# The two ends, the v stage and the u seam of a hybrid RG-LRU / gMLP block: shorter roots, diagonals on ScalarE, constants at the start, operands by tile

## The chip, the cores and the metric

One core of one Trainium2 chip runs the kernel. The metric is the device time of one execution in microseconds (us). A measurement gives the median of several executions.

## The reference, cut to what matters

Batch 1, 1024 tokens, model width 1024, one layer, all in float32:

```python
h = rms_norm(x, norm_mix_g)
rnn_x, rnn_gate, sgu_u, sgu_v, gate_a, gate_b = split(h @ w_in)
rnn_x = causal_depthwise_conv(rnn_x, conv_w, conv_b)
y_a = gelu(rnn_gate) * rg_lru(rnn_x, ...)       # decay = exp(-8 r softplus(-lam))
y_b = gelu(sgu_u) * (tril(w_s) @ layer_norm(gelu(sgu_v)) + b_s)   # chunks of 128 tokens
merged = sigmoid(gate_a) * (y_a @ w_proj_a) + sigmoid(gate_b) * (y_b @ w_proj_b)
x = x + merged @ w_out
g, u = split(rms_norm(x, norm_ffn_g) @ w_gate_up)
x = x + (silu(g) * u) @ w_down
return rms_norm(x, norm_final_g)
```

## The kernel before, in words

**Products.** Each float32 operand is split into a high part, rounded to float32r by ScalarE (ACT, line 93), and a low part, the rest, by VectorE (DVE, line 94). A product is three matmuls on TensorE (PE): high by high, high by low, low by high (`mm3`, lines 97 to 99). The large products after the v stage use a Strassen-Winograd scheme (`wino`, line 232): seven products M1 to M7 of blocks of 512, whose operands A11, A12, A22, S1 to S4 are blocks of the input and sums of them.

**Order of the work.** Weights come through a queue of loads (`start_loads`, line 128, on SyncE's DMA queue, SP) and splits (`pump`, line 136). `state["limit"]` bounds how far it runs and `state["ahead"]` how many splits ahead of their use are made. From line 564 to line 787 the order on PE, ACT, DVE, POOL and SP is the written one (`manual_schedule`). Elsewhere a list scheduler sets it, and `later(n, fn)` puts work n steps on. Every engine and queue works in order, so an instruction that waits holds all behind it.

**Start (lines 567 to 597).** SP loads x transposed (`xt`) in pieces of 256 tokens, the first of them in halves of 128 tokens, and the weights of v's first half, `wv0`. ACT issues the load of `pv`, the small parameters. Twelve warm-up matmuls run on PE. x is scaled by the gain and split (`x_split`); 1/rms of a row is applied later.

**v, first half (lines 594 to 649).** Eight tiles t of 128 tokens, each 24 matmuls. `x_rms` (line 490) makes 1/rms of a pair of tiles from sums of squares, by `rstd_early` (line 394): a root by bits and three Newton steps. `x_diag` (line 495) writes 1/rms on a diagonal, the high parts by ACT (line 500) and the low ones by DVE (line 501), `x_row` (line 505) broadcasts it by a matmul with ones, and `scale_x` (line 513) multiplies x by it. `ws_split` and `ws_sums` prepare the spatial weights. `v0_done` applies Gelu and takes statistics.

**v, second half (lines 708 to 740).** Eight tiles again. Per tile: 24 matmuls with `wv1`, Gelu (line 658), statistics on DVE (line 659). Tiles are grouped as 0, 1-2, 3-4, 5-6, 7. With the last tile of a group come `v_norm` (the root) and `v_centre` (ACT, line 678). Two tiles later `v_split` (lines 684, 685) makes the halves `vn`, `v_mix` multiplies them by the spatial weights (lines 696, 697), ACT copies one part from PSUM (line 699), DVE adds the other (line 705), and SP stores the result to `mix_d` in four pieces of 128 KB. Between these stand the operands of the u products: `scale_x` of x's second half with tiles 0 and 1, `sums` (lines 550 to 552) with tiles 2 and 4, `part` with tiles 1, 2, 4, 5, 6, `sum_s4` with 6 and 7.

**u seam (lines 763 to 786 and 858 to 872).** The first products M1, M2, M5, M6 of u0 and u1 (`head`) alternate with the last two tiles of `v_split` and `v_mix`, with the S2 and S4 parts. S3 and A22 follow outside the written order, and there too the recurrence constants (lines 876 to 892): `lam` is loaded by SP, ACT takes Abs and Exp (line 880), DVE 17 instructions of 128x8.

**After that** come the recurrence and gate products (`rnn_pair`, `gate_pair`), the projections, the feed-forward block and the down product. In the down product (line 1343 on) M4 is the last; after its k loop the four tiles i get their last four k one after the other, and each is then added to x (line 1300), squared (line 1308), multiplied by the gain (line 1310), scaled by its root (`finish`, line 1312) and stored by SP (line 1322). `square` of the second halves comes by `later(8, ...)`.

Of the kernel before, what the change touches and what calls it, by code (L numbers as in the profile page):

```python
# [14 lines left out]
P = 128  # L15
# [13 lines left out]
RG_C = 8.0  # L29

# [21 lines left out]
def block_kernel(ctx: ExitStack, tc: tile.TileContext, a: dict, out: bass.AP):  # L52
# [75 lines left out]
    def start_loads(upto=None):  # L128
        while state["load"] < min(upto or len(loads), state["loads"]) and (state["load"] < 2 or left[state["load"] - 2] == 0):
            ld = loads[state["load"]]  # L130
            ld[2] = wpool.tile([P, 4, HALF], F32, name=f"wraw{state['load']}", tag="wraw")
            for k in range(4) if state["load"] < 2 else (slice(0, ld[1]),):
                nc.sync.dma_start(ld[2][:, k], ld[0][:, k])
# [243 lines left out]
    act.activation(small.tile([P, 1], F32, name="warm", bufs=1), eps_t, AF.Gelu_apprx_tanh)  # L377
# [16 lines left out]
    def rstd_early(pool_, var, scale, name, n=1, y=None):  # L394
# [5 lines left out]
        dve.tensor_scalar(h, var, -0.5 * scale, -0.5 * EPS, ALU.mult, ALU.add)  # L400
        dve.tensor_scalar(y.bitcast(I32), h.bitcast(I32), -0.5, float(0x5F3759DF - 2 ** 22 - 2 ** 30),
                          ALU.mult, ALU.add)
# [56 lines left out]
    with tc.tile_pool(name="phv", bufs=1) as wk:  # L459
# [35 lines left out]
        def x_diag(q):  # L495

            dg = dgs[q] = wk.tile([P, 2, 2, P], F32R, name=f"dg{q}", tag="vb", bufs=3)
            for i in range(2):
                r = rms[:, 2 * q + i:2 * q + i + 1]
                act.activation(dg[:, 0, i], ident, AF.Copy, scale=r)  # L500
                dve.scalar_tensor_tensor(dg[:, 1, i], ident, r, dg[:, 0, i].bitcast(F32), ALU.mult, ALU.subtract)
# [36 lines left out]
        def part(name, src, i):  # L538

            ks = slice(2 * i, 2 * i + 2)  # L540
# [26 lines left out]
        act.dma_start(pv, a["pv"])  # L567
        first, second = slice(0, P), slice(P, 2 * P)
# [873 lines left out]
```

## Time and profile before

| | us |
|---|---|
| median of 3 runs (lowest, highest) | 1420.47 (1419.41, 1421.47) |
| the profiled execution | 1419.23 |
| its span, first to last instruction | 1417.5 |
| PE busy | 1397.0 (99%) |
| PE loading weights, beside it | 1151.0 |
| DVE busy | 1100.7 |
| ACT busy | 792.9 |

Times in rows count from the start of the span. PE's clock has two levels, 2.4 and 1.2 GHz, shown as a granted clock of 1.00 and 0.50. A matmul's row is longer than the distance to the next one, because matmuls are pipelined. "Idle before" is the time that the engine stood before an instruction, with what released it.

### The profile page before, as it was taken

The numbers are of one execution on the slowest core, as the hardware profiler recorded it, in microseconds if no ns is written. First come the engines' busy times: TensorE is split into PE (matmuls) and PEld (weight loads), VectorE is DVE, ScalarE is ACT, GpSimd is POOL, SyncE is SP. The second block draws the span as 40 slices with busy tenths as digits, with TensorE's granted clock in tenths as the row PEclk, the third lists the DMA queues.
The fourth block names the chain that finished last, engine by engine and source line by source line (L and its number), as shares of the span: only waits on it lengthen the run. The fifth ranks groups of instructions, "written<-read, shape, count | busy, mean of one in ns | idle before, by whom it ended". The sixth has DMA issues, their size and how long they took to land.

```text
span 1417.5 us, 17185 instructions
## 1 busy us (share of the span) xinstructions
PE 1397.0 (99%) x6216; PEld 1151.0 (81%) x6216; DVE 1100.7 (78%) x1807; ACT 792.9 (56%) x1320; POOL 75.0 (5%) x59
## 2 busy tenths in 40 slices
PE   9998999999999999999999999999999999999997
PEld 7777888788888888888888788888888888888886
DVE  6999999988888889798656976666666664697595
ACT  8467688888889865443443543333333333444454
POOL 0000000000000000000000021111111111000000
PEclk9999999999999999999999999999999999999999
DMA  9323545433333388774611132222222226942342
GB/s 322 139 60 109 200 164 178 167 116 115 114 107 107 105 310 315 259 295 150 222 60 45 74 112 112 111 112 107 88 110 112 111 93 249 347 179 85 110 141 82
DMA packets 71045, 212.45 MB, mean 150 GB/s; under 512 B 6320, under 2 KB 20656, under 8 KB 58416
## 3 DMA queue, kind: packets, MB, share of 16 engines
q1 hardware_dynamic: 70816, 211.32, 41.7%
q8 instruction: 48, 0.79, 0.2%
q14 instruction: 37, 0.30, 0.1%
q10 hardware_dynamic: 144, 0.04, 0.0%
HBM read 148.68 MB, written 62.65 MB: 149 GB/s over the span
## 4 chain that ended last, share of the span: by engine, by line
PE 73%; DVE 13%; ACT 8%; DMA 2%; issue 2%; SPq 0%; DVEq 0%; ACTq 0%; POOLq 0%; POOL 0%
PE f_p L99 10%; PE f_p L97 10%; PE f_p L98 10%; PE d_M L97 5%; PE d_M L99 5%; PE d_M L98 5%; PE g_p L99 2%; PE g_p L98 2%; PE g_p L97 2%; PE pa_p L98 2%; PE pb_p L99 2%; PE pb_p L98 2%; PE pa_p L97 2%; PE pa_p L99 2%; PE pb_p L97 2%
## 5 line engine op out<-in xcount | busy, mean ns | idle before, releaser
L93 ACT ACTIVATE dl_M<-wraw 128x512 fp32r<-128x512 f32 x77 | 48.6, 631 | 105.0 <-PE d_M L99 92.3
L98 PE MATMUL d_M<-d_M,dl_M 128*128 128x512 f32 x264 | 102.8, 389 | 0.0
L97 PE MATMUL d_M<-d_M,dl_M 128*128 128x512 f32 x264 | 102.7, 389 | 0.0
L99 PE MATMUL d_M<-d_M,dl_M 128*128 128x512 f32 x264 | 102.7, 389 | 0.0
L93 ACT ACTIVATE f_t<-wraw 128x512 fp32r<-128x512 f32 x88 | 55.2, 630 | 84.0 <-PE f_p L99 64.1
L94 DVE TENSOR_TENSOR dl_M<-wraw,dl_M 128x512 fp32r<-128x512 f32 x77 | 54.0, 701 | 51.5 <-ACT dl_M L93 51.3
L94 DVE TENSOR_TENSOR f_t<-wraw,f_t 128x512 fp32r<-128x512 f32 x88 | 70.8, 805 | 23.1 <-ACT f_t L93 22.1
L97 PE MATMUL f_p<-f_S,f_t 128*128 128x512 f32 x176 | 68.6, 390 | 0.3 <-ACT f_t L93 0.3
L97 PE MATMUL f_p<-m,f_b 128*128 128x512 f32 x176 | 68.6, 390 | 0.0
L99 PE MATMUL f_p<-m,f_b 128*128 128x512 f32 x176 | 68.5, 389 | 0.0
L98 PE MATMUL f_p<-f_S,f_t 128*128 128x512 f32 x176 | 68.5, 389 | 0.0
L98 PE MATMUL f_p<-m,f_t 128*128 128x512 f32 x176 | 68.5, 389 | 0.0
L99 PE MATMUL f_p<-m,f_t 128*128 128x512 f32 x176 | 68.5, 389 | 0.0
L98 PE MATMUL f_p<-m,f_b 128*128 128x512 f32 x176 | 68.5, 389 | 0.0
L99 PE MATMUL f_p<-f_S,f_t 128*128 128x512 f32 x176 | 68.4, 390 | 0.0
L97 PE MATMUL f_p<-m,f_t 128*128 128x512 f32 x176 | 68.3, 389 | 0.0
L94 DVE TENSOR_TENSOR f_b<-wraw,f_b 128x512 fp32r<-128x512 f32 x66 | 47.2, 718 | 15.7 <-ACT f_b L93 15.0
L93 ACT ACTIVATE f_b<-wraw 128x512 fp32r<-128x512 f32 x66 | 41.0, 625 | 32.6 <-PE f_p L99 29.9
L98 PEld LDWEIGHTS d_M<-d_M,dl_M 128*128 128x128 f32 x264 | 49.5, 188 | 10.4 <-DVE d_M L94 0.2
L99 PEld LDWEIGHTS d_M<-d_M,dl_M 128*128 128x128 f32 x264 | 49.6, 188 | 10.4
L97 PEld LDWEIGHTS d_M<-d_M,dl_M 128*128 128x128 f32 x264 | 49.5, 188 | 10.3
L198 DVE TENSOR_TENSOR wraw<-wraw 128x512 f32<-128x512 f32 x50 | 53.0, 1060 | 1.1
(503 smaller groups left out, 4208.6 us busy)
## 6 DMA issues: line engine op xcount, KB each, us to landing
wraw<-in_w_gu_dram SPq DMA_DIRECT2D x22, 1024.0 KB, 5.0
wd<-in_w_down_dram SPq DMA_DIRECT2D x11, 1024.0 KB, 9.5
wraw<-in_w_r_dram SPq DMA_DIRECT2D x8, 1024.0 KB, 7.2
wraw<-in_w_g_dram SPq DMA_DIRECT2D x8, 1024.0 KB, 5.0
wraw<-ffs_d SPq DMA_DIRECT2D x8, 1024.0 KB, 5.1
wraw<-ffa_d SPq DMA_DIRECT2D x6, 1024.0 KB, 6.0
xn<-in_x_dram SPq DMA_DIRECT2D x8, 512.0 KB, 9.0
wraw<-in_w_u_dram SPq DMA_DIRECT2D x4, 1024.0 KB, 5.9
```

The lines of the kernel that those rows point to most:

```text
L93: act.activation(hi, src, AF.Copy)
L94: return (eng or dve).tensor_sub(lo, src, hi.bitcast(F32))
L97: pe.matmul(o, lh, rh, start=start, stop=False, **kw)
L98: pe.matmul(o, lh, rl, start=False, stop=False, **kw)
L99: pe.matmul(o, ll, rh, start=False, stop=stop, **kw)
L198: dve.tensor_sub(raw[:, 0], raw[:, 2], raw[:, 0])
```

## The change

- `rstd_early` takes two steps instead of three: an ordinary one and one of higher order; 9 instructions instead of 11 for a pair, 7 instead of 8 for one column.
- `x_diag` splits 1/rms itself (128x2) and ACT writes all four diagonals.
- `lam` is loaded by ACT's queue at the start, right behind `pv`. Abs and Exp stand there ahead of the Gelu warm-up activation, and DVE's 17 instructions behind `x_split(1)`.
- The first loads go weight, x, weight, x, in whole pieces of 256 tokens, and the split of a weight comes before that of x. Eight warm-up matmuls instead of twelve. The first two tiles go k by k.
- The operands are given to other tiles: `scale_x(1)` begins behind tile 6 of the first half; `sums` is cut into `sum_s1`, `sum_s3`, `sum_s2`, with tiles 1, 3 and 5; the S1 parts with tiles 4 and 6; `sum_s4` with tile 7 and in the seam. `v_split` goes by halves, and `mix_out` copies, adds and stores half a tile (256 KB) at a time.
- The seam is written out up to the A22 parts, with each weight split before its head (`ahead` 0).
- At the end the last tile's last four k run in two halves of 256 columns, with partial sums added before; the last root is written out; ACT's queue stores one half. `square` of the second halves comes by `later(5, ...)`.

Cut to its core:

```diff
@@ rstd_early @@
-        for _ in range(3):
-            ...
-            dve.scalar_tensor_tensor(y, t, 1.5, y, ALU.add, ALU.mult)
+        product()
+        dve.scalar_tensor_tensor(y, t, 1.5, y, ALU.add, ALU.mult)
+        product()
+        dve.scalar_tensor_tensor(t, t, 5.0 / 3.0, t, ALU.add, ALU.mult)
+        dve.scalar_tensor_tensor(y, t, 1.25, y, ALU.add, ALU.mult)
@@ x_diag @@
-            act.activation(dg[:, 0, i], ident, AF.Copy, scale=r)
-            dve.scalar_tensor_tensor(dg[:, 1, i], ident, r, dg[:, 0, i].bitcast(F32), ALU.mult, ALU.subtract)
+            split(hi, lo, rms[:, c])
+            for n, r in enumerate((hi.bitcast(F32), lo)):
+                for i in range(2):
+                    act.activation(dg[:, n, i], ident, AF.Copy, scale=r[:, i:i + 1])
@@ start @@
+    act.dma_start(pv, a["pv"])
+    act.dma_start(lam, a["lam"])
...
+        act.activation(lam_c[:, 0], lam, AF.Abs)
+        act.activation(lam_c[:, 0], lam_c[:, 0], AF.Exp, scale=-1.0)
+        act.activation(small.tile([P, 1], F32, name="warm", bufs=1), eps_t, AF.Gelu_apprx_tanh)
+        for j in range(2):
+            ...
+            for k in range(4):
+                nc.sync.dma_start(ld[2][:, k], ld[0][:, k])
+                if j == 0 and k < 2:
+                    xt_load(0, slice(k, k + 1))
+                elif k % 2 == 0:
+                    xt_load(0, slice(4 * j + k, 4 * j + k + 2))
...
-        for _ in range(12):
+        for _ in range(8):
...
-        for ks in (range(4), range(4, 8)):
+        for k in range(NK):
             for t in acc:
-                tm_half(acc[t], "wv0", H, t, ks)
+                tm_half(acc[t], "wv0", H, t, (k,))
...
+        recurrence_constants(wk)
         x_rms(0)
@@ second half of v @@
-            if t == 2:
-                sums(0)
+            if t == 1:
+                part("A11", block(0, 0, 1), 1)
+                sum_s1(0)
+                sum_s3(0)
+                sum_s2(0)
+            if t == 3:
+                sum_s1(1)
+                sum_s3(1)
             if t == 4:
-                part("S1", s1s[0], 0)
-                sums(1)
+                part_s1(0)
...
+            if t == NT - 1:
+                allow(2 * NK + 1)
+                allow(2 * NK + 2)
+                sum_s4(0)
+                part("A12", block(0, 1, 1), 1)
+                v_mix(t - 2)
+                for q in range(2):
+                    mix_out(t - 2, q)
+                    v_split(t - 1, q)
@@ seam @@
         head("u0")
+        pump(where["u0", "M2"] + 1)
         v_mix(6)
-        v_mixed(6)
-        v_split(7)
+        for q in range(2):
+            v_split(7, q)
+            mix_out(6, q)
+        pump(where["u1", "M2"] + 1)
         head("u1")
         take(2)
         head("u0")
+        sums13("u0", raw["u0"])
+        pump(where["u0", "M5"] + 1)
+        sum_s4(1)
+        sums13("u1", raw["u1"])
         v_mix(7)
...
@@ end @@
+    def end(part):
...
+        for i in range(2):
+            c = slice(i * HALF // 2, (i + 1) * HALF // 2)
+            b = ps(f"d_end{i}")[:, c]
+            part(b, c)
+            x = X2[t][:, c]
+            dve.tensor_add(x, x, b)
+            act.activation(b, x, AF.Square, accum_out=q[:, i:i + 1])
...
+        act.activation(o[:, hs(1)], X2[t][:, hs(1)], AF.Copy, scale=s[:, 3:4])
+        act.dma_start(out[ts(t), hs(1)], o[:, hs(1)])
+        dve.tensor_scalar(o[:, hs(0)], o[:, hs(0)], s[:, 3:4], None, ALU.mult)
+        nc.sync.dma_start(out[ts(t), hs(0)], o[:, hs(0)])
...
-            later(8, lambda: square(4 + i, 1))
+            later(5, lambda: square(4 + i, 1))
...
+            if m == "M4" and i == 3:
+                add(banks[c][3], NT - 1, 0)
+                end(part_of)
+                continue
```

## Rows read from the trace of the kernel before

**Rows 1.** Busy us by stretch, with instruction counts; last: PE clock, DMA share, GB/s.

```profile
core 0: us, PE busy (x) PEld busy (x) DVE busy (x) ACT busy (x) POOL busy (x), PEclk, DMA share, GB/s
...
6.40:19.10 12.70, 12.23 (x48) 8.72 (x49) 10.51 (x24) 10.21 (x26) 0.00 (x0) 1.00 1.06 362
...
20.00:54.00 34.00, 33.85 (x153) 27.80 (x152) 29.44 (x94) 24.72 (x53) 1.09 (x1) 1.00 0.62 226
54.00:122.00 68.00, 62.88 (x324) 52.23 (x323) 63.50 (x148) 44.51 (x83) 0.00 (x0) 1.00 0.26 86
122.00:146.00 24.00, 21.89 (x97) 17.63 (x96) 22.01 (x33) 17.23 (x29) 0.10 (x1) 0.93 0.47 143
...
142.20:145.50 3.30, 3.30 (x8) 2.62 (x9) 3.10 (x4) 3.07 (x6) 0.00 (x0) 0.50 0.57 169
...
146.00:260.00 114.00, 113.60 (x500) 93.41 (x499) 109.23 (x188) 86.28 (x127) 0.20 (x2) 1.00 0.56 187
```

**Rows 2.** Timeline of the start (start, us, engine, line); DMA issues, last column us to landing.

```profile
0.80 0.42 ACTq L567 DMA_DIRECT2D pv<-in_pv_dram  x1
...
1.42 4.94 PE L593 MATMUL warm<-ident 128*128 128x128 f32 x24 [1.42 <-POOL ident masks.py:199]
...
6.48 0.50 PE L97 MATMUL pv<-wv,h 128*128 128x512 f32 x1
...
pv<-in_pv_dram ACTq DMA_DIRECT2D x1, 40.0 KB, 2.0
lam<-in_lam_dram SPq DMA_DIRECT2D x1, 4.0 KB, 4.2
```

**Rows 3.** Timeline of the end: the last matmul and DVE behind it.

```profile
1408.41 0.39 PE L99 MATMUL d_M<-d_M,dl_M 128*128 128x512 f32 x1
...
1409.09 0.69 DVE L1310 TENSOR_TENSOR x<-x,g_fin 128x512 f32<-128x512 f32 x1 [0.64 <-ACT g_fin L1308]
...
1409.77 0.67 DVE L1300 TENSOR_TENSOR x<-x,d_M 128x512 f32<-128x512 f32 x1
```

**Rows 4.** Waits of PE: us in total, times, longest.

```profile
PE mx L697 <- DVE vn L685: 2.3, 4, 1.2
PE mx L696 <- ACT vn L684: 2.3, 2, 1.3
PE u_p L97 <- ACT u_t L93: 2.1, 1, 2.1
```

**Rows 5.** Timeline of tile 2 of v's second half, DVE and ACT.

```profile
71.52 0.69 ACT L658 ACTIVATE vb<-pv,rms 128x512 f32<-128x512 f32 x1 [2.59 <-PE pv L99]
...
72.02 1.22 DVE L550 TENSOR_TENSOR xs<-x 128x1024 f32<-128x1024 f32 x1
...
75.67 0.69 DVE L659 BATCH_NORM_STATS2 st<-vb 128x6 f32<-128x512 f32 x1
...
76.84 0.72 ACT L678 ACTIVATE va<-va,mv 128x512 f32<-128x512 f32 x1 [3.15 <-DVE mv L669]
```

**Rows 6.** The root of tiles 1 and 2 on DVE, first and last of 11.

```profile
76.72 0.16 DVE L400 TENSOR_SCALAR rv<-mv 128x2 f32<-128x2 f32 x1
...
78.68 0.16 DVE L409 SCALAR_TENSOR_TENSOR rv<-rv 128x2 f32<-128x2 f32 x1
```

**Rows 7.** The diagonals (busy, mean ns, idle before), and DVE's waits in the seam.

```profile
L501 DVE SCALAR_TENSOR_TENSOR dg<-ident,rms,dg 128x128 fp32r<-128x128 f32 x8 | 2.5, 347 | 1.1 <-ACT dg L500 1.1
...
L500 ACT ACTIVATE dg<-ident,rms 128x128 fp32r<-128x128 f32 x8 | 2.8, 394 | 9.1 <-DVE rms L409 9.1
...
DVE h_S L94 <- ACT h_S L93: 2.2, 4, 1.1
```

**Rows 8.** The constants' load on SP, and ACT's table load and Exp.

```profile
134.89 0.43 SPq L446 DMA_DIRECT2D lam<-in_lam_dram  x1
...
139.38 1.28 ACT L880 ACT_TABLE_LOAD   x1
140.67 0.21 ACT L880 ACTIVATE sp_e<-sp_e 128x8 f32<-128x8 f32 x1
```

**Rows 9.** Two matmuls of 256 columns, and the next one.

```profile
30.05 0.40 PE L511 MATMUL rms<-dg,ones 128*128 128x256 f32 x2
30.28 0.39 PE L97 MATMUL pv<-wv,h 128*128 128x512 f32 x1
```

More of the change, by code (lines that the diff above doesn't have):

```diff
@@ L131, in start_loads @@
             ld[2] = wpool.tile([P, 4, HALF], F32, name=f"wraw{state['load']}", tag="wraw")
-            for k in range(4) if state["load"] < 2 else (slice(0, ld[1]),):
-                nc.sync.dma_start(ld[2][:, k], ld[0][:, k])
+            nc.sync.dma_start(ld[2][:, :ld[1]], ld[0][:, :ld[1]])
             state["load"] += 1
@@ L376, in block_kernel, with recurrence_constants @@
     make_identity(nc, ident)
[L377 removed]
+    lam = const.tile([P, 8], F32, name="lam")
+    lam_c = const.tile([P, 2, 8], F32, name="lam_c")
+    act.dma_start(pv, a["pv"])
+    act.dma_start(lam, a["lam"])
+    def recurrence_constants(wk):
+        sp = {n: wk.tile([P, 8], F32, name=f"sp_{n}") for n in ("z", "z2", "p")}
+        e = lam_c[:, 0]
+        dve.tensor_scalar(sp["z"], e, 2.0, None, ALU.add)
+        dve.reciprocal(sp["z"], sp["z"])
+        dve.tensor_mul(sp["z"], sp["z"], e)
+        dve.tensor_mul(sp["z2"], sp["z"], sp["z"])
+        dve.tensor_scalar(sp["p"], sp["z2"], 1.0 / 17, None, ALU.mult)
+        for c in (15, 13, 11, 9, 7, 5, 3):
+            dve.scalar_tensor_tensor(sp["p"], sp["p"], 1.0 / c, sp["z2"], ALU.add, ALU.mult)
+        dve.scalar_tensor_tensor(sp["p"], sp["p"], 1.0, sp["z"], ALU.add, ALU.mult)
+        dve.tensor_scalar(sp["z"], lam, -1.0, 0.0, ALU.mult, ALU.max)
+        dve.scalar_tensor_tensor(sp["p"], sp["p"], 2.0, sp["z"], ALU.mult, ALU.add)
+        dve.tensor_scalar(lam_c[:, 0], sp["p"], RG_C / 2, None, ALU.mult)
+        dve.tensor_scalar(lam_c[:, 1], sp["p"], -RG_C, None, ALU.mult)
     def par(name, f):
@@ L751, in block_kernel @@
         U = {n: wino(n, ops, *(call(n, i) for i in range(4)), order=LATE) for n in ("u0", "u1")}
-        state["ahead"] = 3
+        raw = {n: loads[queue[where[(n, "M1")]][0]][2] for n in U}
+        state["ahead"] = 0
         def head(n):
@@ L771, in block_kernel @@
         head("u0")
+        sums13("u0", raw["u0"])
+        pump(where["u0", "M5"] + 1)
+        sum_s4(1)
+        sums13("u1", raw["u1"])
         v_mix(7)
-        v_mixed(7)
-        part("S2", block(0, 0, 0), 0)
+        for q in range(2):
+            mix_out(7, q)
+        pump(where["u1", "M5"] + 1)
         head("u1")
-        part("S2", block(0, 0, 1), 1)
+        for i in range(2):
+            part("S2", block(0, 0, i), i)
+        sum2("u0", raw["u0"])
+        pump(where["u0", "M6"] + 1)
+        head("u0")
+        sum2("u1", raw["u1"])
+        pump(where["u1", "M6"] + 1)
+        head("u1")
+        take(4)
+        for i in range(2):
+            part("S4", block(0, 1, i), i)
+        head("u0")
+        head("u1")
+        state["ahead"] = 5
         take(2)
         head("u0")
-        head("u1")
-        part("S4", block(0, 1, 0), 0)
-        take(2)
-        part("S4", block(0, 1, 1), 1)
-        head("u0")
-        head("u1")
-        take(2)
+        a22 = [wk.tile([P, 2, HALF], F32, name=f"a22_{i}", tag="vn", bufs=2) for i in range(2)]
+        for i in range(2):
+            part("S3", block(1, 0, i), i)
+        for i in range(2):
+            act.activation(a22[i], block(1, 1, i), AF.Copy)
+        head("u1")
+        for i in range(2):
+            part("A22", a22[i], i)
         cur["defer"] = False
     ms.__exit__(None, None, None)
+    for fn in postponed:
+        fn()
+    postponed.clear()
     with tc.tile_pool(name="phr", bufs=2) as wk:
@@ L1353, in part, with part_of @@
                     stop and k == KD - 1, skip_group_check=True)
+        def part_of(b, cs):
+            for k in range(last, KD):
+                x, w = weight(("dn", m, k))
+                mm3(b, x[:, 0, ts(3)], x[:, 1, ts(3)], w[:, 0, cs], w[:, 1, cs], k == last, k == KD - 1)
         first = 2 if m == "M4" else 0
```

182 lines of the change are left out of this document (87 added, 95 removed).

## The prediction, made before the change was run

> **What bounds the kernel now.** I read the page's busy shares first: PE works 1397.0 of 1417.5 us, so only about 20 us can be won, and the table by stretch says where. From 146 us on PE is idle 0.4 us in 114 and a matmul of 512 columns comes every 0.227 us (113.6 us over 500) [rows 1]. Idle PE lies at three places. Before the first useful matmul: 6.48 us, in which only warm-up matmuls run [rows 2]. From 54 to 146 us: 68 less 62.88 and 24 less 21.89, 7.2 us in all; DVE is busy 63.50 of the 68, so PE stands because DVE is late. After the last matmul: 8.7 us (1408.80 to 1417.5) [rows 3]. The list of waits names the middle: 2.3 and 2.3 us for `vn`, the halves of the normalized v, and 2.1 us for a weight split of ACT [rows 4]. The last wait costs twice: TensorE's granted clock falls to 0.50, its 1.2 GHz level, for 3.3 us behind it [rows 1], which loses half of that, 1.65 us.
>
> **How the waits for `vn` arise.** ACT has `v1` of tile 2 by 72.2 us, yet DVE's statistics start at 75.67, because three 128x1024 operand passes stand ahead of them. ACT's centring waits 3.15 us for that, and the split of the next tile comes behind it [rows 5]. The root in between is 11 small instructions from 76.72 to 78.84, 0.195 us each [rows 6]. Tile 4 repeats the pattern.
>
> **The change, part by part.**
>
> *Middle (54 to 146).* The sums move from tiles 2 and 4, each of which closes a group, to tiles 1, 3 and 5, which don't: about 3.7 us of DVE work leaves the path from statistics to `vn`. `v_split` and `mix_out` go by half tiles in the last three tiles, so that PE can start on a half. Three pair roots go from 11 to 9 instructions (0.39 us each), two single ones from 8 to 7. Sixteen stores to `mix_d` of twice the size replace 32; on SP only the loads of the seam's `mix` stand behind them, which come later than before. What is to be won is 7.2 us of idle and 1.65 us of half clock, 8.9. Does DVE have the time? It had 63.5 us of work from 54 to 122; it loses 3 x 0.39 + 2 x 0.25 = 1.7 of roots and four 128x512 passes of `scale_x`, 2.8, that go ahead of the loop: 59.0 us into the 62.9 that PE needs. It fits, with 3.9 us for hand-overs. In the seam that follows, splits of operands waited for ACT 2.2 us in four such hand-overs, 0.55 each [rows 7]; I leave three of them on PE's path, 1.6 us. **Term: -7.3.** Ends: -8.9 if none is left, -3.5 if only the wait for ACT's split (2.1 with its 1.65, rounded down) goes.
>
> *Constants.* `lam` was loaded by SP at 134.89 and ACT waited for it, then reloaded its table for 1.28 at 139.38 [rows 8]; PE's 2.1 us wait above stands behind that and is already counted. The 17 small DVE instructions go to about 20 us: 17 x 0.195 = 3.3. From 20 to 54 DVE has 34 less 29.44, 4.6 us free [rows 1]. In come 3.3 and the 2.8 of `scale_x`; out go four roots (4 x 0.39 = 1.6) and eight `dg` passes of 0.347 (2.8, with 1.1 us of waits for ACT) [rows 7] against four tiny subtractions of 0.2. Net +2.5 of 4.6: covered, but the stage becomes full, and if that cover is gone the weights' low halves for the second loop are late; I set 0.3 us.
>
> *Diagonals.* ACT makes four 128x128 copies a pair instead of two: 8 x 0.394 = 3.2 us more, and four tiny ones of 0.2. ACT waited 9.1 us for the roots at this place [rows 7], which covers them: nothing. If DVE were not late there, they would stand ahead of a Gelu, 0.9 us a pair.
>
> *Start.* ACT now issues two DMAs (0.42 each), then waits for `lam`; behind that wait stand the Gelu table load (1.28), the warm activation and `ones` (0.2 and 0.3), and the first weight and x splits (0.63 and 0.5), for which PE and DVE wait. Where will `lam` land? `pv` on this queue took 2.0 us, `lam` on SP's 4.2 [rows 2]; issued at 1.3 it lands at 3.3 to 5.5. I take 3.6, near `pv`, the same queue at the same moment. Abs and Exp 0.4, then the chain above, 2.9: first matmul at 6.9 instead of 6.48. But x comes whole with each weight, so 48 matmuls need 48 x 0.2275 = 10.9 and some 0.6 for the first splits: done at 18.4. Before, the 48 took until 19.1 [rows 1], so -0.7. SP issues 11 loads in another order with the same bytes; queue and engines are the same. **Term with the 0.3: -0.4.** Ends: -1.3, and +3.2 with `lam` at 5.5 (first matmul 2.0 later, at 8.9) and 1.65 of half clock behind an idle PE.
> At the table load a page of the Trainium skill (ScalarE: Activation LUTs, "What ACT_TABLE_LOAD costs") states 1283 ns and a drain of about 1380 for every switch. The trace disagrees on the drain: Exp starts at 140.67, right after 139.38 + 1.28 [rows 8]. By the page the first matmul would come 1.4 us later and the term would be +1.0.
>
> *Recurrence stage (146 to 320).* It loses the 3.3 us of constants on DVE, but PE arrives some 8 us earlier and DVE had only 114 less 109.2, 4.8 us, free until 260 [rows 1]. 4.8 and 3.3 are 8.1: just enough. **Term: +0.5.** Ends: -1.0 (a wait or two fewer) and +3.0 (half of the 4.8 isn't usable, and a hand-over of 0.55).
>
> *End.* The last tile's last four k go in two column halves: 24 matmuls of 256 for 12 of 512, the same columns: two of 256 took 0.23 [rows 9], one of 512 0.227, so 0 (ends -0.1 and +0.5). Before, the add of the last bank started at 1409.77, 0.97 behind PE's end, because DVE had waited for a square of an earlier half [rows 3]; that square now comes three ticks sooner. A half's add, square and multiply save about 0.2 + 0.25; the root is 0.2 shorter; one of two stores goes to ACT's queue, saving one issue (0.42). All of it: 0.97 + 0.45 + 0.2 + 0.4 = 2.0. Against it, DVE gets one more 128x512 add (0.69) and the first half's add and multiply in the last 2.7 us, between tile 6's small instructions; I charge 0.8. **Term: -1.2.** Ends -2.4 and +0.5.
>
> **Sum.** -7.3 - 0.4 + 0.5 - 1.2 = -8.4 us. The profiled execution took 1419.23 us (span 1417.5), 1.24 less than the median shown; laid on it, that is 1410.8, and on the median 1420.47, with which the new runs are compared, **1412.1**.
>
> **The rivals.**
> - *The start loses.* `lam` lands late, and with 8 warm-up matmuls instead of 12 PE stands from 4.6 us (1.42 and two thirds of 4.75, as 12 take some 4.75) to 8.9, and the clock is at 1.2 GHz when it resumes. For: PE stood 2.1 us before the half-clock stretch of the profile [rows 1, 4]. Against: `pv` landed in 2.0 [rows 2]. Start +3.2 instead of -0.4: 1415.7. The Trainium skill (TensorE: Matmul & The Clock Gate, "What's actually happening") says that the throttled state is the default and that activity releases it. By that rule the case could come about even with `lam` early; no row here shows the clock of the first microseconds.
> - *DVE stays the bound.* The waits for `vn` go, and as many come in the seam or the recurrence stage, where DVE's 4.8 us of slack are not where they are needed. For: 109.2 of 114 [rows 1]. Half of the middle, some 4 us, is given back: 1416.1.
> - *The reordering doesn't do what it says.* PE waits for ACT's centring and split, whatever stands ahead on DVE; only the wait for `lam` (2.1 + 1.65) and the end (1.2) are won: 1415.5. Against: ACT waited for DVE there, 3.15 us [rows 5].
> - *Slower.* The seam in written order: each head waits for a split that waits for ACT, in 16 hand-overs, with nothing else allowed in between. It decides from 8.4 / 16 = 0.53 each on, if none is hidden; four were 0.55 on average and one 1.1 [rows 7]. At 0.75 each, 12 us, and two drops of the clock, 3.3, the time is 1420.47 - 8.4 + 15.3 = 1427.4. Against: the order puts the other block's product, 12 matmuls of 0.227, between a split and its use, which hides most.
>
> **How the numbers follow.** Forecast 0.50, late start 0.17, DVE 0.17, reordering 0.10, slower 0.06. A measurement here can tell about 0.2%, 2.8 us, from no change. The forecast and most of the three middle cases are faster by more (4.4 to 8.4 us); a fifth of these three, 0.08, lies within 2.8, and 0.01 goes above: faster 0.85, same 0.08, slower 0.07. Low: all good ends but the recurrence's, -8.9 - 1.3 - 2.4 = -12.6, so 1407.8; high: the three middle cases with a little over 2 us of the bad ends, 1418.
>
> **What would show it.** Right: no wait of PE over 0.6 us for `vn` from 54 to 122, none for ACT's `u_t`, no half-clock stretch after 20 us; the statistics of tile 2 within 1 us of ACT's Gelu; PE's last matmul about 7 us earlier, and 7.5 us from it to the end. Wrong: first useful matmul after 8 us; waits of over 3 us in total in the seam's heads; PE idle from 146 to 320 up by over 2 us; an add of the last half that starts over 1 us behind PE's end.

## The result, and the profile after

The changed kernel takes 1429.09 us (median of 6, 1427.28 to 1431.17), the kernel before beside it 1420.01 (6, 1419.02 to 1421.85): ratio 1.0063, 95% interval 1.0052 to 1.0074. It is slower by 9 us, where 8.4 us less were forecast. The profiled execution took 1430.09 us with a span of 1428.4 (1417.5 before). PE is busy 1401.8 us, 4.8 more at partly half rate; DVE 1098.5, ACT 796.6.

Where it was lost is read from the times at which PE reaches the same work in both traces:

| PE begins (us) | before | after | later by |
|---|---|---|---|
| first useful matmul | 6.48 | 9.37 | 2.9 |
| first row of 1/rms | 30.05 | 33.20 | 3.1 |
| sums of the spatial weights | 47.10 | 54.59 | 7.5 |
| first mix of the second half | 71.32 | 81.17 | 9.9 |
| mix of tile 6 | 117.48 | 122.74 | 5.3 |
| M3 of u | 146.13 | 147.29 | 1.2 |
| first recurrence group | 162.45 | 168.63 | 6.2 |
| second group | 203.39 | 212.05 | 8.7 |
| sixth group | 370.01 | 381.53 | 11.5 |
| end of the span | 1417.5 | 1428.4 | 10.9 |

So PE is 9.9 us late at the first mix, by the start, the first loop and the half rate behind it. 8.7 of these come back in the rest of the second loop and the first part of the seam, and all are lost again, and more, between M3 and the fourth group (299.0 us, 11.3 late). Busy time by stretch after (columns as in [rows 1]):

```profile
core 0: us, PE busy (x) PEld busy (x) DVE busy (x) ACT busy (x) POOL busy (x), PEclk, DMA share, GB/s
...
20.00:54.00 34.00, 31.15 (x139) 25.43 (x138) 25.42 (x90) 25.37 (x62) 1.24 (x1) 1.00 0.64 235
54.00:122.00 68.00, 66.50 (x326) 55.91 (x326) 60.22 (x135) 44.89 (x81) 0.00 (x0) 0.95 0.24 78
122.00:146.00 24.00, 23.33 (x115) 18.74 (x114) 21.61 (x43) 14.14 (x28) 0.00 (x0) 1.00 0.23 67
146.00:260.00 114.00, 109.21 (x466) 87.60 (x465) 105.95 (x166) 89.49 (x131) 0.30 (x3) 0.99 0.56 191
```

Against [rows 1], PE idles less from 54 to 146 (2.2 us for 7.2), as forecast; it idles 2.85 us instead of 0.15 in the first loop and 4.8 instead of 0.4 from 146 on. DVE has less to do in all four rows: it is not busier, it stands. The waits of PE, total, times, longest:

```profile
PE pv L98 <- ACT h L511: 4.2, 1, 4.2
PE pgt L98 <- ACT xs L94: 3.0, 2, 2.4
PE rms L541 <- ACT dg L531: 2.9, 2, 2.7
PE u_p L98 <- ACT h_S L94: 2.3, 1, 2.3
PE r_p L100 <- DVE r_b L95: 1.4, 1, 1.4
```

The waits for `vn` and `u_t` of [rows 4] are gone. In their place ACT is named four times: at the start (`h`), for the diagonals (`dg`), for S3 (`h_S`) and in a gate product (`xs`).

**The start.** Timeline (start, us, engine, line), ACT's queue and ACT, then PE:

```profile
0.80 0.40 ACTq L379 DMA_DIRECT2D pv<-in_pv_dram  x1
1.23 0.46 ACTq L380 DMA_DIRECT2D lam<-in_lam_dram  x1
...
6.23 0.21 ACT L615 ACTIVATE lam_c<-lam 128x8 f32<-128x8 f32 x1 [3.23 <-DMA lam<-in_lam_dram]
...
6.70 1.28 ACT L617 ACT_TABLE_LOAD   x1
...
9.37 0.80 PE L98 MATMUL pv<-wv,h 128*128 128x512 f32 x1 [4.16 <-ACT h L511]
9.96 0.63 PE L99 MATMUL pv<-wv,h 128*128 128x512 f32 x1
10.38 0.63 PE L100 MATMUL pv<-wv,h 128*128 128x512 f32 x1
```

`lam` landed 5.0 us after its issue, and `pv` itself took 4.0 instead of the 2.0 of [rows 2]. Over all runs `pv` took 3.9 to 4.1 us in the seven with the changed order of SP's loads, 2.0 to 3.2 in the eight with the old one; which of the loads beside it makes the difference, no run shows. `lam` behind `pv` took 3.6 to 5.1 in either order. Until 13.4 the matmuls come 0.43 us apart instead of 0.23: half rate, behind 4.16 us in which PE stood.

**The first loop.** Timeline of DVE and ACT at the first pair's diagonals, of DVE's next root, and of PE at the fourth row:

```profile
26.65 3.26 DVE L512 SCALAR_TENSOR_TENSOR h<-x,pv,h 128x256 fp32r<-128x256 f32 x8
26.79 0.19 ACT L94 ACTIVATE rh<-rms 128x2 fp32r<-128x2 f32 x1
27.01 0.70 ACT L531 ACTIVATE dg<-ident,rh 128x128 fp32r<-128x128 f32 x2
29.83 0.15 DVE L95 TENSOR_TENSOR rl<-rms,rh 128x2 f32<-128x2 f32 x1
30.02 0.70 ACT L531 ACTIVATE dg<-ident,rl 128x128 fp32r<-128x128 f32 x2 [2.31 <-DVE rl L95]
...
33.97 0.17 DVE L430 TENSOR_SCALAR rx<-ssqs 128x2 f32<-128x2 f32 x1 [1.37 <-ACT xn L515]
...
53.06 0.39 PE L541 MATMUL rms<-dg,ones 128*128 128x256 f32 x1 [2.65 <-ACT dg L531]
```

The low part of 1/rms is a subtraction of 0.15 us, but in written order it stands behind a pass of 3.26 (`x_split(2)`), and ACT stops for it in the middle of its diagonals. Behind ACT's stop stand the Gelus and the squares; DVE's next root waits 1.37 for these, and ACT for that root in turn. At the fourth row PE waits 2.65 and, with two waits for `ws`, falls to half rate (0.50 from 57.0 to 61.2).

**The seam.** ACT at S3, and the first load of `mix` on SP:

```profile
151.51 0.63 ACT L94 ACTIVATE u_t<-wraw 128x512 fp32r<-128x512 f32 x1 [1.50 <-DVE wraw L227]
...
153.56 0.63 ACT L94 ACTIVATE u_t<-wraw 128x512 fp32r<-128x512 f32 x1 [0.89 <-DVE wraw L227]
154.10 1.99 ACT L94 ACTIVATE h_S<-x 128x1024 fp32r<-128x1024 f32 x2
...
164.40 0.33 SPq L473 DMA_DIRECT2D mix<-mix_d  x1
```

With `ahead` at 5, two later weight splits go ahead of S3 on ACT and wait for sums of DVE; PE waits 2.3 us and drops to half rate once more. And the loads of `mix`, which began at 132.14 before, begin at 164.40: the copies `a22` in the v stage's pool keep its memory until then.

### The profile page after: what moved, and what is told of

Its sections match the earlier page's. It is cut to its first block, busy times and chain, and to the rows that moved or that the text cites. A ratio compares the mean times of both kernels' runs of the same rounds, so it can differ in the third digit from the quotient of the medians.

```text
span 1428.4 us, 17123 instructions
## 1 busy us (share of the span) xinstructions
PE 1401.8 (98%) x6220; PEld 1154.8 (81%) x6220; DVE 1098.5 (77%) x1790; ACT 796.6 (56%) x1332; POOL 75.1 (5%) x59
## 4 chain that ended last, share of the span: by engine, by line
PE 76%; DVE 12%; ACT 8%; issue 2%; DMA 2%; SPq 0%; ACTq 0%; DVEq 0%
PE f_p L100 9%; PE f_p L98 9%; PE f_p L99 9%; PE d_M L99 5%; PE d_M L98 5%; PE d_M L100 5%; PE g_p L98 2%; PE g_p L100 2%; PE g_p L99 2%; PE pa_p L99 2%; PE pb_p L100 2%; PE pb_p L99 2%; PE pa_p L98 2%; PE pa_p L100 2%; PE pb_p L98 2%
## 5 line engine op out<-in xcount | busy, mean ns | idle before, releaser
L99 PE MATMUL d_M<-d_M,dl_M 128*128 128x512 f32 x260 | 101.2, 389 | 0.0
L98 PE MATMUL d_M<-d_M,dl_M 128*128 128x512 f32 x260 | 101.2, 389 | 0.0
L100 PE MATMUL d_M<-d_M,dl_M 128*128 128x512 f32 x260 | 101.1, 389 | 0.0
L98 PE MATMUL pv<-wv,h 128*128 128x512 f32 x128 | 51.8, 405 | 4.2 <-ACT h L511 4.2
```

The source lines that it names most:

```text
L98: pe.matmul(o, lh, rh, start=start, stop=False, **kw)
L99: pe.matmul(o, lh, rl, start=False, stop=False, **kw)
L100: pe.matmul(o, ll, rh, start=False, stop=stop, **kw)
```

## The experiments

All ratios are to the kernel before, run beside on the same chip. The other columns are the times (us) at which PE begins the sums of the spatial weights, the mix of tile 6, and the first, second and sixth recurrence group, from one trace each. The kernels are numbered as the experiments below.

| kernel | median us | ratio (95%) | sums | mix 6 | group 1 | group 2 | group 6 |
|---|---|---|---|---|---|---|---|
| before | | 1 | 47.10 | 117.48 | 162.45 | 203.39 | 370.01 |
| after | 1429.09 | 1.0063 (1.0052, 1.0074) | 54.59 | 122.74 | 168.63 | 212.05 | 381.53 |
| 1 | 1430.93 | 1.0082 (1.0065, 1.0099) | 56.05 | 124.15 | 169.35 | 212.62 | 380.85 |
| 2 | 1431.81 | 1.0087 (1.0072, 1.0102) | 50.97 | 124.78 | 171.96 | 215.05 | 385.13 |
| 3 | 1433.38 | 1.0097 (1.0082, 1.0112) | 53.71 | 121.61 | 160.74 | 216.39 | 385.10 |
| 4 | 1429.42 | 1.0066 (1.0051, 1.0081) | 54.36 | 122.52 | 174.60 | 215.53 | 381.58 |
| 5 | 1429.43 | 1.0056 (1.0041, 1.0071) | 55.22 | 123.39 | 170.34 | 211.28 | 378.91 |
| 6 | 1426.59 | 1.0039 (1.0024, 1.0054) | 48.46 | 120.06 | 165.68 | 209.46 | 379.78 |
| 7 | 1422.58 | 1.0015 (1.0005, 1.0024) | 48.29 | 119.15 | 164.63 | 205.56 | 373.19 |
| 8 | 1428.38 | 1.0060 (1.0046, 1.0073) | 52.36 | 124.83 | 171.96 | 212.89 | 380.34 |
| 9 | 1426.58 | 1.0036 (1.0023, 1.0049) | 51.10 | 121.02 | 166.78 | 210.28 | 378.34 |
| 10 | 1418.42 | 0.9984 (0.9975, 0.9994) | 49.87 | 120.95 | 164.62 | 206.47 | 372.69 |
| 11 | 1417.29 | 0.9980 (0.9971, 0.9989) | 48.31 | 115.52 | 160.41 | 201.38 | 367.76 |
| 12 | 1420.40 | 0.9999 (0.9989, 1.0008) | 47.90 | 112.55 | 160.87 | 201.81 | 372.41 |
| 13 | 1415.63 | 0.9962 (0.9949, 0.9976) | 48.15 | 112.80 | 158.93 | 200.65 | 367.29 |

Single executions of one kernel lie up to 4.8 us apart (9: 1424.67 to 1429.45), so traces give places, and the ratios give sizes. A difference of two ratios is known to some 2 to 2.6 us either way, an estimate from their intervals.

**1. The start alone.** Abs, Exp and a second Gelu warm-up behind the first splits.

```diff
-        act.activation(lam_c[:, 0], lam, AF.Abs)
-        act.activation(lam_c[:, 0], lam_c[:, 0], AF.Exp, scale=-1.0)
...
             x_split(0, (k,))
+        act.activation(lam_c[:, 0], lam, AF.Abs)
+        act.activation(lam_c[:, 0], lam_c[:, 0], AF.Exp, scale=-1.0)
```

> The changed kernel, with Abs, Exp and the Gelu warm-up of the constants behind ACT's first splits instead of ahead of them. Theory (ACT stands until lam lands at 6.23 us, PE idles and resumes at 1.2 GHz): first useful matmul at 6.5 to 7.0 us instead of 9.37, no half-clock stretch from 10 to 13.4 us, and the first row broadcast at 29 to 30.5 instead of 33.2; 3 to 4 us less than the changed kernel's 1429, if the stage behind doesn't take it back. Rival (the new order of loads, weights ahead of x, makes the start late whatever ACT waits for): first matmul still after 8.5 us.

Its timeline of PE:

```profile
6.20 0.80 PE L98 MATMUL pv<-wv,h 128*128 128x512 f32 x1 [0.99 <-ACT h L511]
6.79 0.63 PE L99 MATMUL pv<-wv,h 128*128 128x512 f32 x1
7.22 0.63 PE L100 MATMUL pv<-wv,h 128*128 128x512 f32 x1
```

The first useful matmul comes at 6.20, 3.2 us earlier, yet until 9.4 the steps are 0.43 us: PE had stood only 0.99 us. By the sums of `ws` the gain is gone, PE waits 4.2 us at the fourth row instead of 2.7, and the time is no better, where 3 to 4 us were expected. The start is late, but it hides behind the first loop.

**2. The third and fourth rows of 1/rms back in their old places**, `scale_x(1)` back behind the loop.

```diff
             if t == 5:
                 v0_done(4, acc[4])
-                x_rms(3)
-                x_diag(3)
...
             if t == 6:
                 x_row(2)
-                x_row(3)
+                x_rms(3)
+                x_diag(3)
...
+        x_row(3)
...
-                scale_x(1, range(4, 8))
+                scale_x(1, range(0, 8))
```

> The changed kernel, with squares 6 and 7, the last root, diagonal and row broadcast and the first half of the second scaling in their places of before. Theory (these stand ahead of the spatial weights' split on ACT and DVE, and PE, in order, waits for them in tile 6): the waits of 2.65, 0.56 and 0.91 us at 50 to 56 us fall below 1 us in total and the half clock behind them goes, so the second loop starts 5 to 7 us earlier, of which up to 3 are lost again in the loop because the scaling stands there: 3 to 6 us less than 1429. Rival (the ping-pong of ACT and DVE in the diagonals has made DVE late before): the waits stay over 2 us.

The sums come 3.6 us earlier; then one wait of 4.4 us for `vn` appears at mix 0, since all of `scale_x(1)`, in tile 0 alone, and the sums of tile 1 now stand ahead of that `vn` on DVE. Mix 6 is 2.0 us later than in the changed kernel, and nothing of the gain is left.

**3. S3 ahead of the weight splits. 4. A22 copied in the next pool. 5. Both.**

```diff
+        for i in range(2):
+            part("S3", block(1, 0, i), i)
         state["ahead"] = 5
         take(2)
         head("u0")
-        a22 = [wk.tile([P, 2, HALF], F32, name=f"a22_{i}", tag="vn", bufs=2) for i in range(2)]
```

> The changed kernel, with the two S3 parts ahead of the step that lets weight splits run five ahead. Theory (ACT works in order, and the S3 parts stand behind weight splits of M4 that wait for DVE): PE's wait of 2.25 us before M7 of u0 goes, and with it the half clock from 156.8 to 160.2; 3.5 to 4.5 us less at the start of r0. Rival (DVE is simply full there): the wait moves to M3 or M4, and the gain is under 1.5 us.

> The changed kernel, with the two A22 copies in the next stage's pool and behind the written order, as before. Theory (the copies keep the v stage's memory in use until 163.7 us, so the loads of mix, which use that memory, start only at 164.4, and the outputs of u0 and u1 crowd DVE into the recurrence stage): the loads of mix start about 140 to 150 us, the wait of 1.43 us at r0 goes, and 2 to 5 us are won between r0 and 330 us. Rival (the loads wait for the end of the written order, not for memory): they start at the same place, and the time stays.

> Edit: both changes to the seam together, S3 parts split ahead of the weight splits of M7 and M4, and A22 copied in the next memory pool. Theory (the two single runs failed because each left the other's obstacle in place: S3 first met late loads of `mix` and of the gate weights, A22 in the next pool met a late S3): PE's 2.25 us wait for S3 and its 1.7 us of half clock go, loads of `mix` are issued before 150 us, the first recurrence matmul comes at 161 and the second group at 203 to 207 (212 in the changed kernel): 1422 to 1425. Rival (VectorE's amount of work up to 250 us sets the pace, whatever the order of the seam): the second group stays at 211 to 216 and the time at 1427 to 1432.

S3 first: no wait for S3, and the products with S3 (M7) end at about 157.1 us instead of 163.2. The first group begins 7.9 us earlier, but it now stands ahead of u's last product (M4, from 162.45) and waits 3.5 us for `r_b` at once, so this place is no measure of the gain. The second group begins 4.3 us later, in waits for `r_b`, `r_y` and `r_t`: the loads of `mix` still begin at 164.99. The whole is slower than the changed kernel (1.0097 for 1.0063). A22 in the next pool: they begin at 140.62, but S3 is later still. Both together: 141.20, and the first groups lie 41 us apart, as before the change; the time is that of the changed kernel, as the rival had it. So both readings of the seam are right as mechanisms, and neither they nor the two together carried the 9 us: with both, the first group came at 170.34, now behind waits for weight splits (`u_t`, 1.7 and 1.5).

**6. Start and first loop of before** with the second loop, seam and end of the change; **7. the same with the seam of 5.** Core of 6, against the changed kernel:

```diff
-        act.activation(lam_c[:, 0], lam, AF.Abs)
...
-        for k in range(NK):
-            pump(k + 1)
-            x_split(0, (k,))
+        for k in range(4):
+            x_split(0, (k,), first)
+            pump(k + 1)
...
+        act.activation(lam_c[:, 0], lam, AF.Abs)
...
-        for _ in range(8):
+        for _ in range(12):
...
-                x_diag(1)
                 x_split(3)
+                x_diag(1)
...
-                scale_x(1, range(4, 8))
+                scale_x(1, range(0, 8))
```

> Edit: start and first loop of v as in the kernel before (order of loads, diagonals half on ScalarE and half on VectorE, places of roots, rows and scale_x), with `lam` behind `pv` on ScalarE's queue, Abs and Exp behind the first splits, the 17 constants' instructions where the changed kernel has them, and its shorter roots; second loop, seam and end are those of the changed kernel. Theory (the 10.8 us lost by 58 us come from the start and the hand-overs of the first loop): sums of the spatial weights at 47 to 48.5 us (54.6 changed, 47.1 before), waits for `vn` not over 1 us each, the seam loses what it loses in the changed kernel; steady part 8 to 10 us earlier than in the changed kernel: 1419 to 1422. Rival (VectorE's work is the bound; the lateness of the first loop only shows it early): waits of 2 to 4 us come for `vn` or in the seam, the first recurrence group is under 3 us earlier than in the changed kernel: 1426 to 1430.

> Edit: the two above together, so that of the changed kernel only the shorter roots, the early constants, the second loop of v, the seam with S3 first and A22 late, and the end are left. Theory: first loop as before, no long waits for `vn`, none for `lam` and S3: 1413 to 1418, faster than the kernel before. Rival (VectorE bound): 1420 to 1428.

The sums come at 48.5 and 48.3, 6 us earlier than in the changed kernel, yet mix 6 is 2.6 and 1.7 us later than before the change. Where no wait for `vn` over 1 us was expected, PE waits 4.4 us at mix 0. Kernel 7, timeline of PE:

```profile
76.34 0.33 PE L747 MATMUL mx<-ws,vn 128*128 128x128 f32 x1 [4.44 <-DVE vn L735]
```

Part of this wait is these two runs' own: the last line of the cut puts all eight passes of `scale_x(1)` (5.34 us of DVE) into tile 0, where the kernel before and the changed one have four. The rest seems to come with the change, whose three sums in tile 1 stand ahead of this `vn`: kernel 9 below has `scale_x(1)` in the change's own places and the sums at 51.10, and PE waits there too:

```profile
78.17 0.33 PE L745 MATMUL mx<-ws,vn 128*128 128x128 f32 x1 [1.75 <-DVE vn L733]
```

6 is 3.4 us faster than the changed kernel, and 7 is 5.8 us faster than 5; both lie in the range of their rival, and 7 is slower than the kernel before, where faster was expected. The seam's mending counts 3.4 here (1.0039 to 1.0015) and 1.0 on the changed kernel (1.0063 to 1.0056), and the intervals don't tell these apart.

**8. Only the diagonals on ACT, put into 7. 9. Only the diagonals of before, put into the changed kernel.** Edit of 8, reversed in 9:

```diff
-                act.activation(dg[:, 0, i], ident, AF.Copy, scale=r)
-                dve.scalar_tensor_tensor(dg[:, 1, i], ident, r, dg[:, 0, i].bitcast(F32), ALU.mult, ALU.subtract)
+            split(hi, lo, rms[:, c])
+            for n, r in enumerate((hi.bitcast(F32), lo)):
+                for i in range(2):
+                    act.activation(dg[:, n, i], ident, AF.Copy, scale=r[:, i:i + 1])
```

> Edit: first loop of before with the changed seam mended (1.0015 of the kernel before), and in it only the new diagonals: VectorE subtracts the low part of 1/rms (128x2), ScalarE writes all four diagonals. Theory (the low part stands in written order behind VectorE's pass of x_split, so ScalarE stops at its third diagonal and everything behind it, x's splits and the Gelus, comes later): waits of ScalarE for `rl` of 1 to 2.5 us, the sums of the spatial weights 1 to 3 us later than 48.3, time 1423.5 to 1426. Rival (the prediction's: 3.2 us of ScalarE's work inside its 9.1 us of waits, nothing on the path): 48.3 within 0.5 and 1422 to 1423.

> Edit: the changed kernel with the diagonals of before alone (two copies by ScalarE, two low parts by VectorE a pair). Theory (this hand-over is the largest single loss and adds to the others): the sums of the spatial weights at 49 to 52 us instead of 54.6, no half clock at 57 to 61, 1422 to 1425.5, ratio 1.001 to 1.0035. Rival (the start 2.9 us late and the early third row hold the same instructions, so the gain is masked, as that of the earlier start was): sums at 53 or later, 1427 to 1430.

They cost 1.0060 less 1.0015, 6.4 us, by themselves, more than the theory's range, and taking them out of the changed kernel gives 3.8 us, a little less than expected. This is the largest single edit here; the seam costs more in its two steps together, 3.4 (6 to 7) and 5.3 (12 to 13). Kernel 7, timeline of ACT and DVE:

```profile
26.55 3.26 DVE L513 SCALAR_TENSOR_TENSOR h<-x,pv,h 128x256 fp32r<-128x256 f32 x8
26.65 0.70 ACT L528 ACTIVATE dg<-ident,rms 128x128 fp32r<-128x128 f32 x2
27.25 1.25 ACT L547 ACTIVATE va<-pv,rms 128x512 f32<-128x512 f32 x2
28.39 1.05 ACT L516 ACTIVATE xn<-xn 128x1024 f32<-128x1024 f32 x1
```

Kernel 8, the same place:

```profile
26.41 3.26 DVE L513 SCALAR_TENSOR_TENSOR h<-x,pv,h 128x256 fp32r<-128x256 f32 x8
...
26.74 0.70 ACT L532 ACTIVATE dg<-ident,rh 128x128 fp32r<-128x128 f32 x2
29.58 0.15 DVE L95 TENSOR_TENSOR rl<-rms,rh 128x2 f32<-128x2 f32 x1
29.77 0.69 ACT L532 ACTIVATE dg<-ident,rl 128x128 fp32r<-128x128 f32 x2 [2.33 <-DVE rl L95]
30.37 1.24 ACT L550 ACTIVATE va<-pv,rms 128x512 f32<-128x512 f32 x2
31.51 1.05 ACT L516 ACTIVATE xn<-xn 128x1024 f32<-128x1024 f32 x1
```

Up to 27.3 both engines do the same in both but for `rh`. In 7 ACT goes on to the Gelus, because DVE makes the low diagonals from what ACT has left; in 8 ACT waits until 29.77, and the squares, from which DVE makes the next root, are 3.1 us later (31.51 for 28.39). DVE's busy time from 20 to 54 us falls from 31.06 to 26.39.

**10. The kernel before with two parts of the change: early constants and the new end.**

```diff
         act.dma_start(pv, a["pv"])
+        act.dma_start(lam, a["lam"])
...
+        recurrence_constants(wk)
         x_rms(0)
         x_split(2)
...
+                end(part_of)
```

> Edit: the kernel before with two parts of the change alone: `lam` loaded behind `pv`, Abs and Exp behind the first splits and the 17 instructions behind the first squares, and the new end. By the sum of terms in the prediction: the wait for `u_t` (2.1 us) and its half clock (1.65) go and the end saves 0.75: 1415 to 1416. Rival (what PE gains at 132 us it waits for again in the recurrence stage, where VectorE has no slack): the first recurrence group 3 us earlier, the second at most 1 us earlier than before (203.4), 1418 to 1419.5.

0.9984, 2.3 us: the time lies in the rival's range, but the rival's sign, a first group 3 us earlier, is missing. No waits for `lam` or its `u_t` (0.3 left). The first group is no earlier than before in this trace, though; PE waits at other places (2.2 for a diagonal, 4.5 for `vn`), and it was this kernel's slowest execution.

**11. The same with shorter roots and the operand passes placed behind the statistics**, or into tiles that close no group.

```diff
             v_stats(t, acc)
             if t == group[t][-1]:
                 v_norm(t)
...
+            if t in (2, 4):
+                sum_first(t // 4)
+            if t in (3, 5):
+                part("S1", s1s[t // 4], t // 4)
```

> Edit: the kernel before with early constants and new end (0.9984 of the kernel before), and two more parts of the change in a form of their own: the shorter roots, and in the second loop of v the operand passes placed behind the statistics and the root of a tile or into tiles that close no group (the first sum behind the adds of tiles 2 and 4, the other two ahead of the statistics of 3 and 5, the S1 parts behind the adds of 3 and 5, both A11 parts in tile 1). The first loop, half diagonals, tile-wide splits and the seam's order stay those of before. Theory (in the middle the order on VectorE costs PE, not its amount of work): the waits for `vn`, 4.5 us in five stops in that kernel, fall under 1.5 us, mix 6 comes 2 to 4 us earlier and about half of it lasts: 1415 to 1417. Rival (VectorE's work up to 250 us sets the pace): the first recurrence group gains under 1 us on 164.6, 1417.5 to 1419.

Mix 6 is 5.4 us and the first group 4.2 us earlier than in 10, but the ratio improves by 0.0004 only, inside the intervals; the waits for `vn` did not fall under 1.5 us (4.4: 1.1 at tile 5 and 3.3 at tile 6).

**12. Kernel 7 with the second loop in the order of 11**, splits and stores by half tiles as in the change, `scale_x(1)` in tiles 0 and 1 as before. **13. The same with the seam of before.** Core of 12, against 7:

```diff
-            if t == 0:
-                scale_x(1, range(0, 8))
...
+            if t < 2:
+                scale_x(1, range(4 * t, 4 * t + 4))
...
+            if t in (2, 4):
+                sum_s1(t // 4)
+            if t in (3, 5):
+                part_s1(t // 4)
```

Core of 13, against 12:

```diff
-        state["ahead"] = 0
+        state["ahead"] = 3
...
-        pump(where["u0", "M2"] + 1)
...
-        for i in range(2):
-            part("S3", block(1, 0, i), i)
-        state["ahead"] = 5
...
-        a22 = [wk.tile([P, 2, HALF], F32, name=f"a22_{i}", tag="rr") for i in range(2)]
         for i in range(2):
+            part("S3", block(1, 0, i), i)
```

> Edit: first loop of before, second loop with the operand passes in the order of the fastest kernel so far (0.998), splits and stores by half tiles and the seam in written order with S3 first and A22 late. Theory (the written order itself costs, since each head waits for a split that no other work may pass): no wait for `vn` over 2 us before tile 5, PE idle from 122 to 260 us 4 us or more where the fastest kernel has 1.6, 1419.5 to 1422, ratio 0.9995 to 1.0015. Rival (the seam's waits came from a late second loop): as the fastest kernel, 1416 to 1418.

> Edit: the kernel of the run before with one part undone, the seam: S2, S4, S3 and A22 parts and the weights' splits where the kernel before has them (three splits ahead, S3 and A22 with the list scheduler), while `v_split` and the stores stay by half tiles and the second loop stays as it was. Theory (the written seam order holds back work that is ready, so it costs whatever arrives at it): M5 of u0 at 126 to 127.5 us as in the kernel of the run before, PE idle from 122 to 260 us under 3 us where that has 4.8, no wait of over 1 us for `r_m` and ScalarE's `xs` at 260 us, 1413 to 1416.5, ratio 0.995 to 0.9975. Rival (whatever comes earlier at 126 us waits for VectorE's work before 300 us, in any order): the first recurrence group at 160 us or later, 1417 to 1419.5.

Windows of 12:

```profile
54.00:122.00 68.00, 67.13 (x354) 57.12 (x352) 62.44 (x144) 44.63 (x85) 0.00 (x0) 1.00 0.27 89
122.00:146.00 24.00, 21.50 (x95) 16.38 (x95) 22.08 (x32) 16.79 (x27) 0.10 (x1) 1.00 0.41 122
146.00:260.00 114.00, 111.72 (x481) 90.81 (x479) 106.17 (x169) 80.97 (x122) 0.20 (x2) 0.99 0.56 189
260.00:300.00 40.00, 36.67 (x154) 29.71 (x154) 34.17 (x54) 33.16 (x51) 0.10 (x1) 0.96 0.33 117
```

Windows of 13:

```profile
54.00:122.00 68.00, 67.13 (x352) 57.09 (x351) 62.47 (x145) 43.92 (x83) 0.00 (x0) 1.00 0.26 87
122.00:146.00 24.00, 20.75 (x87) 16.21 (x87) 22.06 (x33) 17.86 (x30) 0.10 (x1) 0.93 0.46 140
146.00:260.00 114.00, 112.40 (x492) 91.73 (x490) 109.08 (x173) 84.13 (x125) 0.20 (x2) 1.00 0.56 189
260.00:300.00 40.00, 39.49 (x173) 32.40 (x174) 35.50 (x57) 32.20 (x50) 0.10 (x1) 1.00 0.43 147
```

From 54 to 122 PE stands 0.87 us of 68 in both, with DVE at 62.4 (63.5 before): the work does fit, and what cost 5.1 us before was its order. It took two parts: 11 has the same operand order with whole-tile splits and stands 4.4 us there, 7 has the half tiles with the change's sums and stands 4.5. The time of 12 is what its theory said (0.9999); the 2.3 us that it gains on 7 include the wait that 7 had brought in itself. 13 is the fastest of all, 0.9962 (0.9949, 0.9976), faster than both kernels of the case, and 5.3 us faster than 12 by the seam alone. The theory had the time right, but not the place. PE idles 4.85 us from 122 to 260 in 13 and 4.78 in 12, where under 3 were expected; at the second group 13 is only 1.2 us ahead, at the third 0.7 (242.33 for 243.02), and then, at the fourth, 4.9 (284.95 for 289.86). Ahead of that, kernel 12, DVE and SP:

```profile
249.04 0.75 DVE L931 SCALAR_TENSOR_TENSOR mix<-mix,pv,sh 128x512 f32<-128x512 f32 x1
...
249.82 0.33 SPq L474 DMA_DIRECT2D graw<-in_rg_w_dram  x1
...
255.29 0.42 ACT L94 ACTIVATE wg<-graw 128x256 fp32r<-128x256 f32 x1 [2.60 <-DMA graw<-in_rg_w_dram]
```

Kernel 13, the same:

```profile
245.80 0.75 DVE L916 SCALAR_TENSOR_TENSOR mix<-mix,pv,sh 128x512 f32<-128x512 f32 x1
...
246.57 0.33 SPq L474 DMA_DIRECT2D graw<-in_rg_w_dram  x1
```

The gate weights `graw` are loaded into the one buffer that `sh` holds, so the load goes out when the last pass that reads `sh` ends. In 12 that pass comes 3.2 us later, ACT waits 2.6 us for the load, DVE 1.8 for ACT, and PE then 1.5 and 1.8 for `r_m` and `xs`, with half rate behind it. That the buffer is what ties them is read from the two traces and the shared tag; no run gave `graw` a buffer of its own. The other traces agree in part. In the four kernels with the seam of before, this load goes out 4.2 us behind the start of the third group, and the fourth group follows the third by 42.6 us; in ten with the written seam it is 6.4 to 6.9 us and 43.6 to 46.8 (6.5 and 45.0 in the changed kernel). But in 4, at 5.1, ACT waits 3.5 us for the load, longer than in 12, and the fourth group still follows by 42.2: the wait of ACT alone does not make PE late. Why the list scheduler gives that pass a later place with the written seam stays open.

## Why the prediction was wrong, and where it was right

Two steps of the sum failed: the diagonals, put at nothing, and the seam, put at 1.6 us. From the changed kernel to the fastest one, the measured ratios give 3.4 us to the start and first loop of before (6), 3.4 to S3 and A22 (7), 2.3 to the second loop (12) and 5.3 to the rest of the seam's order (13): 14.3 us, 8.7 of them in the seam.

- **Middle, with the seam.** The waits for `vn` are gone from the changed kernel, but in part by luck: PE is 9.9 us late at the first mix there, and when it comes earlier it waits for `vn` again (1.75 us in 9). That DVE has the time is shown by 12, in another order. The 1.6 us for three hand-overs in the seam is the part that was mis-sized: S3 alone took 2.3 and 1.6 of half rate behind it (157.0 to 160.2 at 0.50), because I followed the order of the parts but not that `ahead` at 5 pumps two weight splits onto ACT ahead of S3. That the copies `a22` keep the v stage's memory, and so hold back the loads of `mix` for 32 us, was not in the sum at all, and neither was the 5.3 us that the rest of the written seam costs (13).
- **Diagonals: as one step, this failed most.** "ACT waited 9.1 us for the roots at this place [rows 7], which covers them: nothing." The busy time was covered; the extra hand-over from ACT to DVE and back was not, and it stands behind a 3.26 us pass. Run 8 prices it at 6.4 us.
- **Constants and DVE's slack.** "Net +2.5 of 4.6: covered, but the stage becomes full." It became emptier: DVE is busy 25.42 of 34, and PE stands. The idle time between dependent hand-overs was no slack to put work into. On the kernel before, the early constants and the new end together gain 2.3 us (10), about half of what their terms had promised.
- **Start.** The bad end came true: +3.2 was its bound, with the first matmul at 8.9; 9.37 was measured, and PE is 3.1 us late at the first row. The step that failed is `lam`'s landing, put at 3.6 us, near `pv`; it landed at 6.23. In all 14 runs that load it on this queue it landed behind `pv`, and in the old order of loads too it took 3.6 to 5.1 us. (SP issues 13 loads here, not 11.) The rival for it came true at the place and the rate, but run 1 shows that its price hid behind the first loop, and that an early `lam` would not have saved the rate with 8 warm-up matmuls.
- **Recurrence.** +0.5 with ends -1.0 to +3.0. From the first to the sixth group it took 212.9 us instead of 207.6: +5.3. PE did not arrive early on a DVE with slack; it arrived 6.2 us late and waited on the way, 1.4 us for `r_b` and 3.0 for `xs`.
- **End.** -1.2 was forecast, 0.9 measured: from the start of the last matmul (1420.31, before 1408.41) to the end of the span 8.1 us instead of 9.1, less 0.1 for the shorter matmul. The last half's add starts 0.5 us behind PE's end, under the 1 us that would have shown the term wrong.
- **The slower rival** had the sign, and with 1427.4 nearly the time, partly by luck. It priced the waits in the seam's heads; PE stands 0.7 us from 122 to 146, where most of them lie. The seam did cost, but behind them: at S3, in the loads of `mix`, and in the recurrence stage (13). The diagonals it doesn't name: in the first loop ACT and DVE wait for each other in turn, and PE pays only at the fourth row.
- **Signs.** Of the signs of being wrong, two came: the first matmul after 8 us, and PE's idle time from 146 to 320, 7.5 us for 1.8. The waits in the heads and the late last add did not.
- **Table load and clock.** ACT's table load at 6.70 took 1.28 and the next activation began at 7.99, so nothing was lost behind it. The Trainium skill (ScalarE: Activation LUTs, "What ACT_TABLE_LOAD costs") gives a drain of about 1380 ns there; the trace shows none, again. PE ran at half rate from 9.96 to 13.4 behind its idle time, and in run 1 behind 0.99 us of it. The Trainium skill (TensorE: Matmul & The Clock Gate, "What's actually happening") has the throttled state as the default; the trace agrees.

Gains did not add: the start (run 1) and the rows (2) gained 3.2 and 3.6 us at their own places, S3 (3) about 5 by the end of M7, and none of them gained anything at the end. The gains that lasted came in kernels with the diagonals or the first loop of before (6, 7, 9, 12, 13). What the change's own second loop does behind that first loop, with `scale_x(1)` in its own places, no run shows.

## What to carry to other kernels

Price a hand-over, not an instruction: before you call moved work hidden, write down which long pass it stands behind on the other engine, and who stands behind the waiting one. An engine's idle time counts as slack only if the work put there depends on nothing that the neighbour has yet to do. When a run takes one part back, look for a wait that the run itself brings in before you read its time. Where a part is reordered, follow what its buffers hold back, since a load that goes out when a buffer comes free can be late a whole stage further on.

## What the runs showed of the hardware

The granted clock of the profile doesn't show half rate in the first microseconds. Windows of the changed kernel:

```profile
10.00:13.40 3.40, 3.40 (x10) 2.62 (x9) 3.40 (x8) 3.40 (x8) 0.00 (x0) 1.00 0.89 289
57.00:61.20 4.20, 4.20 (x12) 3.23 (x11) 4.07 (x12) 1.26 (x2) 0.00 (x0) 0.50 0.27 103
```

Both stretches have matmuls 0.43 us apart, the 1.2 GHz level, and only the second is given with 0.50. With 12 warm-up matmuls, whose last ends 0.1 us ahead of the first useful one [rows 2], the steps are 0.23 to 0.34 at once, apart from waits; with 8 and 0.99 us of idle they are 0.43 until 9.4. And a load of 4 KB, issued behind one of 40 KB on the same queue and beside SP's first loads, took 3.6 to 5.1 us to land in the 14 runs that have it so, the one of 40 KB 2.0 to 4.1.
